# The last 256 columns of an output projection made one tile of 128 at a time, and the results written in smaller pieces from three engines

## The chip, the cores and the metric

The kernel runs on one core of a Trainium2 chip. The metric is the device time of one execution in microseconds (us), as the median of several runs. TensorE (PE in the profile) multiplies, VectorE (DVE), ScalarE (ACT) and GpSimd (POOL) work elementwise, SyncE (SP) starts transfers; ACT can start transfers too, and all transfers share 16 DMA engines.

## The reference, cut to what matters

One layer of a streaming encoder serves 256 prompt rows and 32 sample rows with the same weights (D = 2048). The change concerns its last two lines alone:

```
out = merged @ w_out                      # 288 rows x 2048 @ 2048 x 2048, float32
x   = x + gate * rms_norm(out, g_post)    # mean of squares over the 2048 columns, then 1/sqrt
```

## The kernel before, in words

All 288 rows (`T`) stand side by side as the moving operand, transposed, and weights are the stationary operand, so that a product comes out as tiles of 128 output columns by 288 rows. Each float32 factor is split into a high part and a rest, which gives three products: `hi` by `xh` (L161), `hi` by `xl` (L162) and `lo` by `xh` (L164). `weights` (L137) loads 8 x 128 rows by 256 columns (1 MB, tile `raw`) from SP's queue; `split_weights` (L144) cuts it into two pieces of four 128-row blocks each, `whi` with a copy on ACT (L126) and `wlo` with a subtraction on DVE (L127). `product` (L176) makes 256 columns (`WC`), which are two output tiles, f = 0 and f = 1, in two PSUM tiles `acc`: over four pieces it runs the 12 matmuls of f = 0 and then the 12 of f = 1 for each piece, so both tiles are complete only with the last piece.

The output projection is the loop at L793 over q = 0 to 7, 256 columns each. After the product, each tile is copied to SBUF (`of`, L800, ACT), transposed by PE into the PSUM tiles `aux` (L804 for the two groups of 128 prompt rows, L806 for the samples), squared and summed along its columns by ACT (L810, the sum goes to `so`), and multiplied by the gate `gbc` on DVE (L822) into the result buffers: `t` for the prompts, the second half of `xt` for the samples. At q = 6 DVE sums the seven finished parts of the squares (`sm`, L814 and L815); at q = 7 it adds the last (L817), and GpSimd raises `sm` to the power of -0.5 (`rr`, L819). Then DVE makes `x + t * rr` in one instruction for each half of each prompt group (four of 128x1024) and one for the samples (32x2048, `xt`), all at L828; each result is stored by a transfer that ACT starts (L830: `p % 2` is 0 for all five).

The order on the engines at this point is set by a scheduler from the program's order and its dependences, not by hand. There are four `acc` and four `aux` tiles in PSUM, and four buffers each of `whi` and `wlo`.

Of the kernel before, what the change touches and what calls it, by code (L numbers as in the profile page):

```python
# [10 lines left out]
F32 = mybir.dt.float32  # L11
F32R = mybir.dt.float32r
AF = mybir.ActivationFunctionType
ALU = mybir.AluOpType
PSUM = bass.MemoryType.PSUM

P = 128
# [89 lines left out]
def hybrid_step(ctx: ExitStack, tc, x_prompt, x_sample, c_prompt, c_sample, state_conv, state_ret,  # L107
# [13 lines left out]
    def acc_tile():  # L121
        return acc.tile([P, 512], F32, name="acc", tag="acc")
# [21 lines left out]
    def split_weights(raw):  # L144

        n, width = raw.shape[1:]
        m = min(n, PIECE // width)
        for k in range(0, n, m):
            m = min(m, n - k)
            hi = buffer("whi", PIECE, F32R, PARTS, MORE_PARTS)  # L150
            lo = buffer("wlo", PIECE, F32R, PARTS, MORE_PARTS)
            hi, lo = (t[:, :m * width].rearrange("p (k c) -> p k c", k=m) for t in (hi, lo))
            split(raw[:, k:k + m], hi, lo)
            yield k, hi, lo
# [21 lines left out]
    def product(w, col, xh, xl):  # L176

        out = [acc_tile(), acc_tile()]
        for half in range(2):
            for k, hi, lo in split_weights(weights(w, half * KH, KH, col, WC)):  # L180
                kt = half * KH + k
                for f in range(2):
                    accumulate(out[f][:, :T], hi, lo, f, kt, xh, xl, kt == 0, kt + hi.shape[1] == NK)
                    step()
                    if between and kt == KH and f == 0:
                        between.pop(0)()
            turn[0] += 1
            if turn[0] % 2 == 0:
                next(later, None)
        return [o[:, :T] for o in out]  # L190

    ident = const.tile([P, P], F32, name="ident")
    make_identity(nc, ident)
# [589 lines left out]
    with tc.tile_pool(name="fin", bufs=2, reuse_waits="tile") as fp:  # L783
        so = fp.tile([P, 3, NQ], F32, name="so", bufs=1)
        V.memset(so, 1.0)
        x01 = ybig.tile([P, 2, D], F32, name="x01", tag="yh")
        t01 = pbig.tile([P, 2, D], F32, name="t01", tag="part")
        xt2 = ybig.tile([P, 2, D], F32, name="xt2", tag="yl")
        xs = (x01[:, 0, :], x01[:, 1, :], xt2[:, 0, :])
        ts = (t01[:, 0, :], t01[:, 1, :], xt2[:, 1, :])  # L790
        A.dma_start(out=x01, in_=x_prompt[0].rearrange("(g p) d -> p g d", p=P))
        A.dma_start(out=xs[2][:TS], in_=x_sample[0])
        for q in range(NQ):  # L793
            cols = slice(q * WC, (q + 1) * WC)
            pm = product(w_out[0], q * WC, mh, ml)
            pa, pb = aux_tile(), aux_tile()
            os = []
            for f in range(2):
                o = fp.tile([P, T], F32, name="of")
                A.copy(out=o, in_=pm[f][:, :T])  # L800
                os.append(o)
            for f, o in enumerate(os):
                for g in range(2):
                    nc.tensor.transpose(out=pa[:, g * WC + f * P:g * WC + (f + 1) * P], in_=o[:, g * P:(g + 1) * P], identity=ident)  # L804
            for f, o in enumerate(os):
                nc.tensor.transpose(out=pb[:TS, f * P:(f + 1) * P], in_=o[:, TP:T], identity=ident)  # L806
            src = (pa[:, 0:WC], pa[:, WC:2 * WC], pb[:TS, 0:WC])
            for g in range(3):
                n = rows_of[g]
                A.activation(ts[g][:n, cols], src[g], AF.Square, accum_out=so[:n, g, q:q + 1])  # L810
            if q == NQ - 2:

                sm = fp.tile([P, 3], F32, name="sm", bufs=1)
                V.tensor_reduce(out=sm, in_=so[:, :, :NQ - 1], axis=mybir.AxisListType.X, op=ALU.add)  # L814
                V.tensor_scalar(out=sm, in0=sm, scalar1=1.0 / D, scalar2=EPS, op0=ALU.mult, op1=ALU.add)  # L815
            if q == NQ - 1:
                V.scalar_tensor_tensor(out=sm, in0=so[:, :, q], scalar=1.0 / D, in1=sm, op0=ALU.mult, op1=ALU.add)  # L817
                rr = fp.tile([P, 3], F32, name="rr", bufs=1)
                G.tensor_tensor(out=rr, in0=sm, in1=neghalf, op=ALU.pow)  # L819
            for g in range(3):  # L820
                n = rows_of[g]
                V.tensor_tensor(out=ts[g][:n, cols], in0=src[g], in1=gbc[:n, 0 if g < 2 else 1, cols], op=ALU.mult)  # L822
        outs = (y_prompt[0, 0:P], y_prompt[0, P:TP], y_sample[0])
        W = D // 4
        for g, p, w in ((0, 0, 2), (0, 2, 2), (1, 0, 2), (1, 2, 2), (2, 0, 4)):
            n = rows_of[g]
            c = slice(p * W, (p + w) * W)
            V.scalar_tensor_tensor(out=xs[g][:n, c], in0=ts[g][:n, c], scalar=rr[:n, g:g + 1], in1=xs[g][:n, c],  # L828
                                   op0=ALU.mult, op1=ALU.add)
            (nc.sync if p % 2 else A).dma_start(out=outs[g][:, c], in_=xs[g][:n, c])  # L830


_INS = ["x_prompt", "x_sample", "c_prompt", "c_sample", "state_conv", "state_ret", "ada_w", "ada_b", "norm_pre",
# [28 lines left out]
```

## Time and profile before

| what | value |
|---|---|
| time, median of 3 runs | 1353.85 us (1353.58 to 1354.37) |
| the profiled execution's own time | 1354.2 us |
| its span, first to last instruction | 1352.4 us |
| PE busy | 1324.2 us, 98% of the span |
| DVE, ACT, POOL busy | 834.1, 547.5, 10.0 us |
| moved by DMA | 267.80 MB, mean 198 GB/s |

The span is what the profile's rows cover; 1.8 us of the profiled execution lie outside of it. Rows are given in us from the span's start. A duration of a pipelined instruction runs from its start to its end, so that two neighbours overlap; where a sequence is added up, the distance of starts counts.

### The profile page before, as it was taken

To read this page: it belongs to the slowest core of one execution; us is meant where nothing else is said; L and a number is where in the kernel's file an instruction comes from. 1 tells how busy PE (TensorE), PEld (TensorE's weight loads), DVE (VectorE), ACT (ScalarE), POOL (GpSimd) and SP (SyncE) were. 2 spreads that over 40 slices of the span, in tenths; PEclk is the share of its full clock that TensorE was granted. 3 is DMA by queue.
4 is the path that set the end of the run, shared out by engine and by line. 5 is a ranking of instruction groups with operands and counts; after the bars stand their busy time and mean duration, and the time that the engine had idled before them with its cause. 6 is when DMAs were issued, how large, how long until landed. Compare 5 with 4: busy or idle time off the path is not lost.

```text
span 1352.4 us, 24163 instructions
## 1 busy us (share of the span) xinstructions
PE 1324.2 (98%) x10266; PEld 1302.0 (96%) x10266; DVE 834.1 (62%) x1380; ACT 547.5 (40%) x812; POOL 10.0 (1%) x18
## 2 busy tenths in 40 slices
PE   6999999999999999999999999999999999999996
PEld 5899899999999999999999999999999999999995
DVE  4667679865557766756877875555555544655443
ACT  4443346654444333333333333333333334334441
POOL 0000000000000000000000000000000000000000
PEclk8999999999999999999999999999999999999998
DMA  9988765455455675675666665544546355557431
GB/s 381 376 320 332 298 226 163 129 164 166 144 172 172 211 249 187 200 236 188 199 208 217 203 207 183 180 163 157 183 160 188 126 173 170 157 169 244 156 94 70
DMA packets 209116, 267.80 MB, mean 198 GB/s; under 512 B 5072, under 2 KB 199936, under 8 KB 201872
## 3 DMA queue, kind: packets, MB, share of 16 engines
q1 hardware_dynamic: 202784, 256.13, 55.9%
q10 hardware_dynamic: 6224, 10.13, 2.5%
q8 instruction: 80, 1.31, 0.4%
q14 instruction: 28, 0.23, 0.1%
HBM read 261.75 MB, written 4.49 MB: 197 GB/s over the span
## 4 chain that ended last, share of the span: by engine, by line
PE 96%; DVE 2%; ACT 1%; DMA 1%; issue 0%; DVEq 0%; POOL 0%; POOLq 0%; ACTq 0%
PE acc L162 26%; PE acc L161 26%; PE acc L164 26%; PE pair L374 4%; PE pair L378 4%; PE pair L375 4%; PE small L306 2%; PE aux L665 1%; PE aux L508 0%; PE aux L509 0%; PE aux L510 0%; DVE wlo L289 0%; PE pair L422 0%; PE aux L610 0%; DMA state<-in_state_ret_dram 0%; PE aux L804 0%
## 5 line engine op out<-in xcount | busy, mean ns | idle before, releaser
L127 DVE TENSOR_TENSOR wlo<-raw,whi 128x1024 fp32r<-128x1024 f32 x336 | 410.4, 1222 | 364.6 <-ACT whi L126 364.3
L126 ACT CAST whi<-raw 128x1024 fp32r<-128x1024 f32 x336 | 352.6, 1050 | 518.6 <-PE acc L162 471.3
L161 PE MATMUL acc<-hh,whi 128*128 128x288 f32 x1920 | 524.4, 296 | 0.9 <-DVE firsts L383 0.9
L162 PE MATMUL acc<-hl,whi 128*128 128x288 f32 x1920 | 525.0, 295 | 0.0
L161 PEld LDWEIGHTS acc<-hh,whi 128*128 128x128 f32 x1920 | 360.8, 188 | 1.4 <-ACT whi L126 1.1
L162 PEld LDWEIGHTS acc<-hl,whi 128*128 128x128 f32 x1920 | 361.1, 188 | 0.1
L164 PE MATMUL acc<-hh,wlo 128*128 128x288 f32 x1920 | 329.4, 293 | 0.0
L164 PEld LDWEIGHTS acc<-hh,wlo 128*128 128x128 f32 x1920 | 281.1, 188 | 0.0
L374 PE MATMUL pair<-hh,whi 128*128 128x288 f32 x384 | 110.3, 302 | 2.3 <-ACT hh L346 1.7
L375 PE MATMUL pair<-hl,whi 128*128 128x288 f32 x384 | 109.1, 299 | 0.1
L649 DVE SCALAR_TENSOR_TENSOR gbc<-raw,sc,gbc 128x256 f32<-128x256 f32 x240 | 100.5, 476 | 4.0 <-DMA raw<-in_ada_w_dram 3.9
L383 DVE TENSOR_TENSOR firsts<-pair,firsts 128x576 f32<-128x576 f32 x84 | 62.3, 753 | 39.4 <-PE pair L378 39.3
L378 PE MATMUL pair<-hh,wlo 128*128 128x288 f32 x384 | 84.1, 299 | 1.9 <-DVE wlo L289 1.8
L374 PEld LDWEIGHTS pair<-hh,whi 128*128 128x128 f32 x384 | 73.3, 191 | 5.8 <-issue 2.9
L375 PEld LDWEIGHTS pair<-hl,whi 128*128 128x128 f32 x384 | 73.4, 191 | 0.3 <-DVE hl L352 0.3
L162 PE MATMUL acc<-ml,whi 128*128 128x288 f32 x256 | 70.6, 297 | 0.0
L161 PE MATMUL acc<-mh,whi 128*128 128x288 f32 x256 | 70.1, 296 | 0.0
L161 PE MATMUL acc<-ch,whi 128*128 128x288 f32 x256 | 70.0, 296 | 0.0
L162 PE MATMUL acc<-yl,whi 128*128 128x288 f32 x256 | 70.0, 295 | 0.0
L161 PE MATMUL acc<-yh,whi 128*128 128x288 f32 x256 | 69.9, 296 | 0.0
L162 PE MATMUL acc<-cl,whi 128*128 128x288 f32 x256 | 69.5, 294 | 0.0
L378 PEld LDWEIGHTS pair<-hh,wlo 128*128 128x128 f32 x384 | 63.0, 191 | 3.1 <-DVE wlo L289 3.1
(182 smaller groups left out, 1316.3 us busy)
## 6 DMA issues: line engine op xcount, KB each, us to landing
raw<-in_w_in_dram SPq DMA_DIRECT2D x120, 1024.0 KB
raw<-in_w_branch_dram SPq DMA_DIRECT2D x32, 1024.0 KB
raw<-in_ada_first_dram SPq DMA_DIRECT2D x28, 1024.0 KB
raw<-in_w_first_dram SPq DMA_DIRECT2D x23, 1024.0 KB
raw<-in_ada_w_dram SPq DMA_DIRECT2D x16, 1024.0 KB
raw<-in_w_out_dram SPq DMA_DIRECT2D x16, 1024.0 KB
raw<-in_ada_first_dram SPq DMA_DIRECT2D x8, 512.0 KB
raw<-in_x_prompt_dram SPq DMA_DIRECT2D x2, 1024.0 KB
```

Source lines behind the costliest of these rows:

```text
L126: A.copy(out=hi, in_=src)
L127: V.tensor_tensor(out=lo, in0=src, in1=hi.bitcast(F32), op=ALU.subtract)
L161: nc.tensor.matmul(ps, hi[:, k, fs], xh[:, k0 + k, :], start=first and k == 0, stop=False)
L162: nc.tensor.matmul(ps, hi[:, k, fs], xl[:, k0 + k, :], start=False, stop=False)
L164: nc.tensor.matmul(ps, lo[:, k, fs], xh[:, k0 + k, :], start=False, stop=last and k == n - 1)
L306: nc.tensor.matmul(pm[at:at + 32, :GS * P], cs[:, kt, :], v[:, k, s, :], start=kt < 2, stop=kt >= NK - 2, tile_position=(0, at))
L374: nc.tensor.matmul(ps, hi[:, fs], hh[:, kt, :], start=k == 0, stop=False)
L375: nc.tensor.matmul(ps, hi[:, fs], hl[:, kt, :], start=False, stop=False)
L378: nc.tensor.matmul(ps, lo[:, fs], hh[:, kt, :], start=False, stop=k == GS - 1)
L383: V.tensor_tensor(out=sums, in0=pp[:, :, :T], in1=sums, op=ALU.add)
L649: V.scalar_tensor_tensor(out=ga[:, b], in0=raw[:, k], scalar=sc[:, kt, b:b + 1], in1=ga[:, b], op0=ALU.mult, op1=ALU.add)
L665: nc.tensor.matmul(pg[:, b, :], ones32, ga[:, b, :], start=True, stop=True)
```

## The change

The loop now stops after q = 6. The last 256 columns go through `product_by_tile`: it loads and splits the same four pieces, then runs all 48 matmuls of f = 0, hands that tile out, and runs the 48 of f = 1. Copy, transposes, squares and gate are made for each tile apart, 128 columns wide. At the end the prompts' result is made on DVE in pieces of 512, 768, 768, 1024 and 1024 columns and stored from SP's queue; the samples' result is made in two halves of 1024 columns, the product with `rr` on ACT (Identity with a scale) and the sum with `x` on GpSimd, and stored from ACT's queue.

```diff
+    def product_by_tile(w, col, xh, xl):
+
+        out = [acc_tile(), acc_tile()]
+        pieces = [(half * KH + k, hi, lo) for half in range(2) for k, hi, lo in split_weights(weights(w, half * KH, KH, col, WC))]
+        for f in range(2):
+            for kt, hi, lo in pieces:
+                accumulate(out[f][:, :T], hi, lo, f, kt, xh, xl, kt == 0, kt + hi.shape[1] == NK)
+            yield out[f][:, :T]
...
-        for q in range(NQ):
+        def turned(f, ps, pa, pb):
+
+            o = fp.tile([P, T], F32, name="of")
+            A.copy(out=o, in_=ps)
+            for g in range(2):
+                nc.tensor.transpose(out=pa[:, g * WC + f * P:g * WC + (f + 1) * P], in_=o[:, g * P:(g + 1) * P], identity=ident)
+            nc.tensor.transpose(out=pb[:TS, f * P:(f + 1) * P], in_=o[:, TP:T], identity=ident)
+
+
+        sl = fp.tile([P, 3, 2], F32, name="sl", bufs=1)
+        V.memset(sl, 0.0)
+        for q in range(NQ - 1):
...
+        q = NQ - 1
+        for f, ps in enumerate(product_by_tile(w_out[0], q * WC, mh, ml)):
+            pa, pb = aux_tile(), aux_tile()
+            turned(0, ps, pa, pb)
+            cols = slice(q * WC + f * P, q * WC + (f + 1) * P)
+            src = (pa[:, 0:P], pa[:, WC:WC + P], pb[:TS, 0:P])
+            for g in range(3):
+                n = rows_of[g]
+                A.activation(ts[g][:n, cols], src[g], AF.Square, accum_out=sl[:n, g, f:f + 1])
+            V.scalar_tensor_tensor(out=sm, in0=sl[:, :, f], scalar=1.0 / D, in1=sm, op0=ALU.mult, op1=ALU.add)
+            if f == 1:
                 rr = fp.tile([P, 3], F32, name="rr", bufs=1)
                 G.tensor_tensor(out=rr, in0=sm, in1=neghalf, op=ALU.pow)
             for g in range(3):
                 n = rows_of[g]
                 V.tensor_tensor(out=ts[g][:n, cols], in0=src[g], in1=gbc[:n, 0 if g < 2 else 1, cols], op=ALU.mult)
         outs = (y_prompt[0, 0:P], y_prompt[0, P:TP], y_sample[0])
-        W = D // 4
-        for g, p, w in ((0, 0, 2), (0, 2, 2), (1, 0, 2), (1, 2, 2), (2, 0, 4)):
+        W = D // 8
+
+        def result(g, p, w):
             n = rows_of[g]
             c = slice(p * W, (p + w) * W)
-            V.scalar_tensor_tensor(out=xs[g][:n, c], in0=ts[g][:n, c], scalar=rr[:n, g:g + 1], in1=xs[g][:n, c],
-                                   op0=ALU.mult, op1=ALU.add)
-            (nc.sync if p % 2 else A).dma_start(out=outs[g][:, c], in_=xs[g][:n, c])
+            if g < 2:
+                V.scalar_tensor_tensor(out=xs[g][:n, c], in0=ts[g][:n, c], scalar=rr[:n, g:g + 1], in1=xs[g][:n, c],
+                                       op0=ALU.mult, op1=ALU.add)
+            else:
+                A.activation(ts[g][:n, c], ts[g][:n, c], AF.Identity, scale=rr[:n, g:g + 1])
+                G.tensor_tensor(out=xs[g][:n, c], in0=ts[g][:n, c], in1=xs[g][:n, c], op=ALU.add)
+            (nc.sync if g < 2 else A).dma_start(out=outs[g][:, c], in_=xs[g][:n, c])
+
+        for g, p, w in ((0, 0, 2), (2, 0, 4), (2, 4, 4), (0, 2, 3), (0, 5, 3), (1, 0, 4), (1, 4, 4)):
+            result(g, p, w)
```

The order of the instructions differs from before in the tail alone. On PE, the kernel before ends as follows; acc_14133 is the tile of f = 1 at q = 7, of_14252 and of_14254 are the copies of f = 0 and f = 1.

```order
L161 MATMUL acc_14133<-mh_12156,whi_14222 128x288
L162 MATMUL acc_14133<-ml_12157,whi_14222 128x288
L164 MATMUL acc_14133<-mh_12156,wlo_14223 128x288 x4
L804 MATMUL aux_14250<-ident_67,of_14252 128x128 x2
L806 MATMUL aux_14251<-ident_67,of_14252 32x128
L804 MATMUL aux_14250<-ident_67,of_14254 128x128 x2
L806 MATMUL aux_14251<-ident_67,of_14254 32x128
```

In the changed kernel the place that differs on PE is where f = 0 (acc_14134) ends and f = 1 (acc_14135) begins; of_14206 is the copy of f = 0.

```order
L162 MATMUL acc_14134<-ml_12157,whi_14152 128x288
L164 MATMUL acc_14134<-mh_12156,wlo_14153 128x288 x4
L161 MATMUL acc_14135<-mh_12156,whi_14138 128x288
L162 MATMUL acc_14135<-ml_12157,whi_14138 128x288
L161 MATMUL acc_14135<-mh_12156,whi_14138 128x288
L162 MATMUL acc_14135<-ml_12157,whi_14138 128x288
L807 MATMUL aux_14204<-ident_67,of_14206 128x128 x2
L808 MATMUL aux_14205<-ident_67,of_14206 32x128
L161 MATMUL acc_14135<-mh_12156,whi_14138 128x288
```

The three transposes of f = 0 have moved from the tail to the fifth place of f = 1's accumulation; the tail keeps those of f = 1.

On DVE, the kernel before ends with one gate product for each group, the sum of squares, and the five results.

```order
L822 TENSOR_TENSOR t_13173<-aux,gbc 128x256
L817 SCALAR_TENSOR_TENSOR sm<-so,sm 128x3
L822 TENSOR_TENSOR t_13173<-aux,gbc 128x256
L822 TENSOR_TENSOR xt_13174<-aux,gbc 32x256
L828 SCALAR_TENSOR_TENSOR x_13172<-t_13173,rr,x_13172 128x1024 x4
L828 SCALAR_TENSOR_TENSOR xt_13174<-xt_13174,rr 32x2048
```

In the changed kernel DVE's end from the last column tile on reads:

```order
L847 TENSOR_TENSOR t_13173<-aux,gbc 128x128
L841 SCALAR_TENSOR_TENSOR sm<-sl,sm 128x3
L847 TENSOR_TENSOR t_13173<-aux,gbc 128x128
L847 TENSOR_TENSOR xt_13174<-aux,gbc 32x128
L855 SCALAR_TENSOR_TENSOR x_13172<-t_13173,rr,x_13172 128x512
L855 SCALAR_TENSOR_TENSOR x_13172<-t_13173,rr,x_13172 128x768 x2
L855 SCALAR_TENSOR_TENSOR x_13172<-t_13173,rr,x_13172 128x1024 x2
```

The samples' instruction has left DVE, and the prompts' first piece has half its former columns. On ACT, the changed kernel ends as follows (before, ACT ended with the three squares of 256 columns and five DMA issues).

```order
L805 COPY of<-acc 128x288
L840 ACTIVATE t_13173,sl<-aux 128x128 x2
L840 ACTIVATE xt_13174,sl<-aux 32x128
L858 ACTIVATE xt_13174<-xt_13174,rr 32x1024 x2
L860 DMA out_dram<-xt_13174 32x1024 x2
```

The samples' two products with `rr` have come onto ACT, with their two stores behind them; GpSimd has two sums `xt<-xt` of 32x1024 (L859) behind `rr`, and SP the five prompt stores behind its last weight load.

## Rows read from the trace of the kernel before

**Rows 1.** The page's first part: busy time, share of the span and instructions of each engine.

```profile
PE 1324.2 (98%) x10266; PEld 1302.0 (96%) x10266; DVE 834.1 (62%) x1380; ACT 547.5 (40%) x812; POOL 10.0 (1%) x18
```

**Rows 2.** The chain of waits that ended last, in order of time, over the last 15 us: start, duration, engine and what it worked on.

```profile
1337.63 0.53 PE acc L164 x4
...
1338.24 0.41 ACT of L800
...
1338.69 0.45 PE aux L804 x2
...
1339.16 0.84 ACT t L810 x4
1340.01 0.35 ACT xt L810 x2
...
1340.38 0.17 DVE sm L817
...
1340.66 0.89 POOLq L858
...
1341.57 1.28 DVE x L828
```

**Rows 3.** The timeline of the same stretch: start, duration, engine, line, operation, out<-in, sizes; in brackets the idle time before and who ended it.

```profile
1336.67 0.40 ACT L800 COPY of<-acc 128x288 f32<-128x288 f32 x1 [9.38 <-PE acc L164]
...
1337.98 0.38 PE L804 MATMUL aux<-ident,of 128*128 128x128 f32 x2
...
1340.04 0.42 DVE L822 TENSOR_TENSOR t<-aux,gbc 128x256 f32<-128x256 f32 x1 [11.82 <-ACT t L810]
```

**Rows 4.** The timeline of PE (PEld is its weight load) where the transposes of q = 6 stand between matmuls of q = 7.

```profile
1324.04 0.68 PE L164 MATMUL acc<-mh,wlo 128*128 128x288 f32 x4
...
1324.55 0.38 PE L804 MATMUL aux<-ident,of 128*128 128x128 f32 x2
...
1324.80 0.38 PE L161 MATMUL acc<-mh,whi 128*128 128x288 f32 x1
...
1325.41 0.29 PE L161 MATMUL acc<-mh,whi 128*128 128x288 f32 x1
1325.63 0.20 PEld L804 LDWEIGHTS aux<-ident,of 128*128 128x128 f32 x2 [0.17 <-ACT of L800]
...
1325.94 0.38 PE L162 MATMUL acc<-ml,whi 128*128 128x288 f32 x1
```

**Rows 5.** The timeline of ACT and DVE where the last of the four weight pieces of q = 7 is split.

```profile
1324.23 1.05 ACT L126 CAST whi<-raw 128x1024 fp32r<-128x1024 f32 x1 [0.59 <-PE acc L162]
...
1325.31 1.22 DVE L127 TENSOR_TENSOR wlo<-raw,whi 128x1024 fp32r<-128x1024 f32 x1 [1.94 <-ACT whi L126]
```

**Rows 6.** The instructions of L828 (duration in ns, least, median and most; first and last start), and the four of the prompts in the timeline.

```profile
L828 DVE SCALAR_TENSOR_TENSOR x<-t,rr,x x4: 1276/1277/1283, 1341.6 to 1345.2; 128x1024 f32<-128x1024 f32 x4
L828 DVE SCALAR_TENSOR_TENSOR xt<-xt,rr x1: 2333/2333/2333, 1346.4 to 1346.4; 32x2048 f32<-32x2048 f32 x1
...
1341.57 4.87 DVE L828 SCALAR_TENSOR_TENSOR x<-t,rr,x 128x1024 f32<-128x1024 f32 x4 [0.38 <-POOL rr L819]
```

**Rows 7.** The stores: their issues on ACT's queue in the timeline; then stretches of the span with, behind each, its length, the busy time of PE, PEld, DVE, ACT and POOL, the granted clock of PE, the busy share of the DMA engines and GB/s.

```profile
1342.88 3.92 ACTq L830 DMA_DIRECT2D out_dram<-x  x4
1348.72 0.34 ACTq L830 DMA_DIRECT2D out_dram<-xt  x1
...
1342.88:1343.76 0.88, 0.00 (x0) 0.00 (x0) 0.88 (x1) 0.00 (x0) 0.00 (x0) 0.65 0.00 0
1343.76:1349.10 5.34, 0.00 (x0) 0.00 (x0) 4.93 (x4) 0.00 (x0) 0.00 (x0) 0.50 0.99 393
1349.56:1350.96 1.40, 0.00 (x0) 0.00 (x0) 0.00 (x0) 0.00 (x0) 0.00 (x0) 0.50 0.88 187
1350.96:1352.40 1.44, 0.00 (x0) 0.00 (x0) 0.00 (x0) 0.00 (x0) 0.00 (x0) 0.50 0.00 0
```

**Rows 8.** SP's last weight load: its issue in the timeline, and the stretch of 1 us behind it (columns as in rows 7).

```profile
1299.70 0.37 SPq L141 DMA_DIRECT2D raw<-in_w_out_dram  x1
...
1299.70:1300.70 1.00, 1.00 (x10) 1.00 (x9) 0.58 (x2) 0.72 (x5) 0.00 (x0) 1.00 0.00 0
```

**Rows 9.** Groups of instructions on ACT by line and shape: count, busy us, mean ns of one, idle before.

```profile
L345 ACT ACTIVATE h<-xT,add,mul 128x256 f32<-128x256 f32 x15 | 9.0, 600 | 9.6 <-DVE add L330 9.6
L810 ACT ACTIVATE t<-aux 128x256 f32<-128x256 f32 x16 | 6.0, 381 | 4.4 <-PE aux L804 4.4
L345 ACT ACTIVATE h<-xT,add,mul 128x32 f32<-128x32 f32 x14 | 5.6, 399 | 0.0
L126 ACT CAST vh<-aux 128x512 fp32r<-128x512 f32 x8 | 4.7, 586 | 1.1 <-PE aux L554 1.1
```

**Rows 10.** The same for POOL; these are nearly all that it does.

```profile
L204 POOL TENSOR_TENSOR rstd<-ms,neghalf 128x3 f32<-128x3 f32 x8 | 6.8, 851 | 401.0 <-DVE so L596 341.0 <-DVE ms L202 60.0
L204 POOL TENSOR_TENSOR rstd<-ms,neghalf 128x1 f32<-128x1 f32 x3 | 1.7, 559 | 9.5 <-DVE pick L214 5.3 <-DVE ms L202 4.2
...
masks.py:199 POOL TENSOR_SCALAR_AFFINE_SELECT ident<-ident 128x128 f32<-128x128 f32 x1 | 0.3, 293 | 0.1
masks.py:197 POOL MEMSET ident<- 128x128 f32 x1 | 0.2, 204 | 0.3 <-POOLq L843 0.3
...
L843 POOL MEMSET const-float32-1.0<- 128x1 f32 x1 | 0.1, 99 | 0.0
```

More of the change, by code (lines that the diff above doesn't have):

```diff
@@ L796, in hybrid_step @@
             pa, pb = aux_tile(), aux_tile()
-            os = []
             for f in range(2):
[L799 to L806, printed above, removed]
+                turned(f, pm[f], pa, pb)
             src = (pa[:, 0:WC], pa[:, WC:2 * WC], pb[:TS, 0:WC])
@@ L815, in hybrid_step @@
                 V.tensor_scalar(out=sm, in0=sm, scalar1=1.0 / D, scalar2=EPS, op0=ALU.mult, op1=ALU.add)
-            if q == NQ - 1:
-                V.scalar_tensor_tensor(out=sm, in0=so[:, :, q], scalar=1.0 / D, in1=sm, op0=ALU.mult, op1=ALU.add)
+            for g in range(3):
+                n = rows_of[g]
+                V.tensor_tensor(out=ts[g][:n, cols], in0=src[g], in1=gbc[:n, 0 if g < 2 else 1, cols], op=ALU.mult)
+        q = NQ - 1
[4 more added lines that the diff above has]
+            src = (pa[:, 0:P], pa[:, WC:WC + P], pb[:TS, 0:P])
+            for g in range(3):
+                n = rows_of[g]
+                A.activation(ts[g][:n, cols], src[g], AF.Square, accum_out=sl[:n, g, f:f + 1])
+            V.scalar_tensor_tensor(out=sm, in0=sl[:, :, f], scalar=1.0 / D, in1=sm, op0=ALU.mult, op1=ALU.add)
+            if f == 1:
                 rr = fp.tile([P, 3], F32, name="rr", bufs=1)
```

## The prediction

> **What bounds the kernel now.** I read the busy times first: PE works for 98% of the span [rows 1], so an edit can only count where PE waits, or has finished. The change touches the last 15 us. The chain of waits there shows the second place: PE's last accumulation ends at 1338.16, and from then on one engine works at a time [rows 2]: ACT copies (to 1338.65), PE transposes (to 1339.14), ACT squares (to 1340.36), DVE and POOL make `rr` (to 1341.55), and from 1341.57 DVE makes the results. I call this start S. S lies 3.41 us behind PE's last accumulation. Then the stores: the first is issued when DVE's first piece is done, its data moves from 1343.76, and the 16 DMA engines are 99% busy at 393 GB/s until 1349.10 [rows 7]. DVE makes a prompt piece of 512 KB in 1.20 us from start to start ((1345.2-1341.6)/3, [rows 6]), 437 GB/s, a little faster than the stores drain. The samples' 256 KB come last: DVE needs 2.33 us for them [rows 6], so the DMA engines stand idle for 0.46 us, and then move them at 187 GB/s in 1.40 us. From there to the span's end it is 1.44 us [rows 7]. So the tail has three sections: PE's end to S (bound by a chain), S to the first data (one DVE piece and one issue), first to last data (7.20 us; bound by DMA, and at its end by DVE).
>
> **The change part by part.**
>
> *PE, f = 0's transposes.* Before, they lie under the copy of f = 1: from 1337.98, done long before that copy lets the next ones start [rows 3, 2]; they cost nothing. Now they stand in the midst of f = 1's matmuls, with the whole of PE's stream behind them. Matmuls start every 0.13 us (0.53 for four, rows 2). At q = 6 three transposes lengthen the distance of two matmuls to 0.37 (1324.80 less 1324.43, the fourth start of that L164 group), 0.24 more, where their copy was ready, and to 0.53, 0.40 more, where PE waited 0.17 for it [rows 4]. The new ones stand four matmuls, 0.52 us, behind f = 0's last; its copy is ready 0.53 us (1338.69 less 1338.16) behind that matmul's end, which lies 0.16 behind the start of the next. So there is a wait of about 0.17 again. I take **+0.40**; ends +0.24 and +0.55.
>
> *The order of matmuls.* f = 0 now takes a weight piece every 1.58 us instead of every 3.16, so the last piece is needed three pieces behind the start of q = 7 at 1324.80, at about 1329.9. It is split by 1326.53 (1325.31 plus 1.22, [rows 5]): 3.4 us of cover, and no cost. Without that cover PE would wait for the difference. Copy, squares and gate of f = 0 lie under f = 1's 6.3 us on engines that had idled 9.4 and 11.8 us there [rows 3].
>
> *PE's end to S.* The three squares have 128 columns less each. ACT from PSUM takes 381 ns for 256 columns and 586 for 512, 0.80 ns a column [rows 9], so 0.10 each: **-0.31**; ends -0.20 (part of it fixed) and -0.35. The first gate product on DVE stands ahead of the sum; it shrinks as well (from 0.42, rows 3) and stays beside the third square. S becomes 1341.57+0.40-0.31 = 1341.66.
>
> *First store.* DVE takes 1277 ns for 1024 columns and 2333 for 2048, 1.03 ns a column, so 749 for 512: **-0.53**. The store moves to SP's queue, which has nothing else left. SP's last load shows no byte for 1.00 us behind its issue [rows 8], ACT's first store 0.88 [rows 7]: **+0.16** with the 1.04 I take; ends 0 and 0.2. First data at S+1.82 (0.75 and 0.03 to the issue).
>
> *DVE.* Starts follow each other 0.08 closer than the durations; pieces of 512, 768, 768, 1024, 1024 start at S, 0.67, 1.60, 2.53 and 3.73, and the last ends at **S+5.01**. Before it was 1348.69, S+7.12: the samples' 2.33 have left it. The last store's data can move from S+6.08.
>
> *Samples.* ACT's product of 1024 columns with a scale: L345 gives 0.90 ns a column and 370 fixed, 1.29 us; a plain copy 1.05 [rows 5, 9]; I take 1.25. GpSimd's sum of 1024 columns has no row. Its fill of 128 columns takes 204 ns against 99 for one, 0.82 ns a column, which would be 0.94 us for the sum; its select, one read and one write, 293 ns, 1.5 a column, 1.6 us; with two reads twice that, 3.2 us [rows 10]. Two columns more of the power cost 292 ns, 146 each, which would be 150 us; that is a function's price and not a sum's, and I leave it out. I take 2.3, between select and twice select. Then the halves are ready at S+3.6 and S+5.9, and the second one's data can move at S+6.8, while the last prompt store moves. This path sets nothing as long as its last data moves by S+7.4. The Trainium skill (GPSIMD Engine Reference, section "3.1 Elementwise — side-by-side cycle accounting") gives 4497 ns for a sum of 2048 float32 columns; halved, an estimate of 2.25 us, by which the sum would not change. No row here shows it.
>
> *First to last data.* The bytes are the same 2.36 MB; at 393 GB/s they need 6.0 us. The second store comes 0.26 late (its piece ends at S+1.68, data at S+2.75, the first is moved by S+2.49); after that data always waits. So 6.3 us where it was 7.20: **-0.90**; ends -1.2 (no gap) and -0.5 (the samples' last half on its own at 187 GB/s, 0.70 us). The drain is now the bound, and DVE's last piece, done 2 us before its last byte, is not.
>
> *Sum.* +0.40-0.31-0.53+0.16-0.90 = **-1.18 us**; with all the ends taken together -1.8 to -0.3. The profiled execution has a span of 1352.4 and 1354.2 of its own time, so 1351.2 and 1353.0; that execution lies 0.35 over the median, so for the median 1353.85-1.18 = **1352.65**, own range 1352.1 to 1353.5.
>
> **The rivals.**
>
> *DVE and GpSimd keep each other from SBUF.* Both read two operands from SBUF at that moment, L855 its `t` and `x`, L859 its product and `x`. No row of before has the two engines so at once: GpSimd's powers run while DVE waits for them, and the last one beside products that read one operand from PSUM. If only one of them can read at a time, DVE's 5.0 us and GpSimd's 4.6 stand in line. With the sums in between: the first asks at S+1.3, runs from the end of DVE's second piece at 1.68 to 3.98, the third piece to 4.99, the second sum to 7.29, the last pieces to S+9.77; then 1.07 to data, 1.33 for 512 KB, 1.44 to the end: S+13.6 = 1355.3, **+2.9**, 1356.7. With both sums behind DVE: S+9.6, 0.91 to data, 0.70, 1.44: S+12.65 = 1354.3, **+1.9**, 1355.75. With a sum of 1.6 us it would be 1.4 less. It decides from the point at which DVE's last piece is 0.7 us late (data over by S+8.1), and the gain is gone at 1.9 us. For it: the operands; against it: nothing but that no row shows it. This is the case on the other side: 34%, 1355.4 to 1356.8, likeliest 1356.3. The Trainium skill (SBUF — State Buffer, section "Who interferes with whom") speaks for it: a DVE instruction with two SBUF inputs contends with a GpSimd instruction that reads SBUF, and the one that issues first holds the shared ports for its whole length. By that rule the first time of this paragraph would come out; the trace cannot agree or disagree.
>
> *They only slow each other*, each by a part: between both cases, about +0.7, 1354.5: 12%.
>
> *GpSimd's sum is slow.* At 3.2 us, without any quarrel, the halves end at S+4.5 and S+7.7, the last data moves from S+8.6 for 0.7: S+10.75, 1352.4, no change, 1353.85: 10%. That is the edit that takes work off DVE and puts as much on a slower path.
>
> *The change does less than it says*: the scheduler could have left f = 0's transposes at the end; its order shows that it did not. They could gain nothing where the copy is late: if ACT were busy, PE would wait there longer, up to 0.5 more; ACT has no piece left to split then [rows 5], so I give it no chance of its own.
>
> **How the numbers follow.** The forecast has 44%, the rivals 34, 12 and 10. A change of 0.2%, 2.7 us, is about what a measurement of this kernel can tell from none. Faster than 1351.1 would need more than all ends on the good side: 3%. Slower than 1356.55 holds about a third of the first rival and a little for what I have not thought of: 14%. The rest, 83%, is within. The range reaches from the forecast's low side, 1351.9, to the first rival's high side, 1356.8; no more than 1 in 10 is outside.
>
> **What the profile of the changed kernel would show.** PE's last accumulation about 0.4 later than 1338.16; S 3.1 behind it; the first prompt piece 0.75 us long, five pieces without idle time between, the last done 5.0 us behind S; sums of GpSimd near 2.3 us each beside them; the DMA engines busy from S+1.8 to S+8.1 with one short gap. If a prompt piece of DVE starts late or lasts 2 us and more, or a sum of GpSimd lasts far over 2.3 while DVE works, the first rival has it. If the sums last over 3 us and DVE is undisturbed, it is the slow sum. A last weight piece that PE waits for, or a first store that takes much over 1 us to its data, would make the sum wrong at a place where I see no reason for it.

## The result and the profile after

The changed kernel takes 1357.04 us (median of 17 runs, 1356.28 to 1358.07) and the kernel before 1354.34 on the same chip (17 runs, 1353.44 to 1355.62): ratio 1.0021, interval 1.0015 to 1.0028. It is slower by 2.7 us. The forecast was 1352.65; the time lies just above the range, and what came is the first rival. The profiled execution has a span of 1354.49 where before's has 1352.41.

The busy times, with [rows 1] beside them, show it in one place only: PE, DVE and ACT differ by 3 us or less, and POOL has gained 5.7 us with two instructions more.

```profile
PE 1324.2 (98%) x10266; PEld 1301.6 (96%) x10266; DVE 837.1 (62%) x1385; ACT 550.0 (41%) x820; POOL 15.7 (1%) x20
```

The chain of waits of the last 15 us (start, duration, engine and what it worked on), to be read with [rows 2]:

```profile
1337.98 0.54 PE acc L164 x4
...
1338.60 0.41 ACT of L805
...
1339.05 0.45 PE aux L807 x2
...
1339.53 0.63 ACT t L840 x4
1340.15 0.24 ACT xt L840 x2
...
1340.73 0.85 POOL rr L844
...
1341.61 0.75 DVE x L855
1342.36 0.93 DVEq L891
1343.29 7.49 DVE x L855 x3
```

Up to the start of the results, S, the links are those of before. PE ends at 1338.51 (1337.98 plus 0.54, less 0.01 of rounding) and S is 1341.61, so it is 3.10 us long and was 3.42. The two squares of the prompts and that of the samples take 0.63 and 0.24 where they took 0.84 and 0.35. The new thing is the last line: three pieces of DVE last 7.49 us.

DVE's pieces one by one in the timeline (start, duration, line, out<-in, sizes; in brackets the idle time before):

```profile
1341.61 0.75 DVE L855 SCALAR_TENSOR_TENSOR x<-t,rr,x 128x512 f32<-128x512 f32 x1 [0.65 <-POOL rr L844]
1342.28 1.01 DVE L855 SCALAR_TENSOR_TENSOR x<-t,rr,x 128x768 f32<-128x768 f32 x1
1343.21 3.10 DVE L855 SCALAR_TENSOR_TENSOR x<-t,rr,x 128x768 f32<-128x768 f32 x1
1346.23 3.35 DVE L855 SCALAR_TENSOR_TENSOR x<-t,rr,x 128x1024 f32<-128x1024 f32 x1
1349.51 1.27 DVE L855 SCALAR_TENSOR_TENSOR x<-t,rr,x 128x1024 f32<-128x1024 f32 x1
```

and GpSimd's two sums in the same stretch:

```profile
1342.83 2.66 POOL L859 TENSOR_TENSOR xt<-xt 32x1024 f32<-32x1024 f32 x1 [1.26 <-ACT xt L858]
1345.46 3.04 POOL L859 TENSOR_TENSOR xt<-xt 32x1024 f32<-32x1024 f32 x1
```

Lay the ends side by side. DVE's second piece ends at 1343.29; the first sum, which was there since 1342.83, ends 2.20 later, at 1345.49. DVE's third piece, there since 1343.21, ends 0.82 after that, at 1346.31. The second sum ends 2.19 after that (1348.50), the fourth piece 1.08 after that (1349.58). Each engine finishes one instruction while the other stands: they take turns, by whole instructions. Two pieces of the same shape differ by a factor of about three (768 columns: 1.01 and 3.10; 1024 columns: 1.27 and 3.35), so it is not the pieces' own work.

The stores follow. In stretches of the span (behind each its length, the busy time of PE, PEld, DVE, ACT and POOL, PE's clock, the busy share of the DMA engines and GB/s):

```profile
1343.24:1345.00 1.76, 0.00 (x0) 0.00 (x0) 1.76 (x2) 0.55 (x1) 1.76 (x1) 0.70 0.88 339
1345.00:1347.20 2.20, 0.00 (x0) 0.00 (x0) 2.20 (x2) 0.00 (x0) 2.20 (x2) 0.50 0.37 96
1347.20:1350.40 3.20, 0.00 (x0) 0.00 (x0) 3.20 (x2) 0.00 (x0) 1.30 (x1) 0.50 0.48 157
1350.40:1353.18 2.78, 0.00 (x0) 0.00 (x0) 0.38 (x1) 0.00 (x0) 0.00 (x0) 0.50 0.94 377
1353.18:1354.49 1.31, 0.00 (x0) 0.00 (x0) 0.00 (x0) 0.00 (x0) 0.00 (x0) 0.50 0.00 0
```

In [rows 7] the DMA engines had 5.34 us without a gap at 393 GB/s; now they wait for data in the middle, at 96 and 157 GB/s. The last data moves at 1353.18, 11.57 us behind S (9.40 before). So the 2.07 us of the two spans are: S later by 0.04 (PE's end +0.36, the way from there to S -0.32), S to last data +2.17, last data to end -0.13.

### The profile page after: what moved, and what is told of

It is laid out like the page before. It is cut to its first block, busy times and chain, and to the rows that moved or that the text cites. A ratio compares the mean times of both kernels' runs of the same rounds, so it can differ in the third digit from the quotient of the medians.

```text
span 1354.5 us, 24188 instructions
## 1 busy us (share of the span) xinstructions
PE 1324.2 (98%) x10266; PEld 1301.6 (96%) x10266; DVE 837.1 (62%) x1385; ACT 550.0 (41%) x820; POOL 15.7 (1%) x20
## 4 chain that ended last, share of the span: by engine, by line
PE 96%; DVE 2%; ACT 1%; DMA 1%; issue 0%; POOL 0%; DVEq 0%; POOLq 0%; ACTq 0%
PE acc L161 26%; PE acc L162 26%; PE acc L164 26%; PE pair L383 4%; PE pair L387 4%; PE pair L384 4%; PE small L315 2%; DVE x L855 1%; PE aux L674 1%; PE aux L517 0%; PE aux L518 0%; PE aux L519 0%; DVE wlo L298 0%; PE pair L431 0%; PE aux L807 0%; PE aux L619 0%
```

## The experiments

In the expectations, theory A is that VectorE's and GpSimd's instructions with operands in SBUF exclude each other for their whole length; theory B is that the stores or ScalarE's product hold VectorE up. Where an excerpt of a diff leaves lines out, `...` stands for them.

**Both kernels a second time.**

> The kernel before, unchanged, for a second profile. In the profiles so far a group of 12 matmuls of the output projection takes 1568 and 1591 ns in turn in the kernel before, and 1600 in the changed one in the loops that the change left alone; over five loops that is 0.78 us. If that belongs to the run and not to the program, this profile shows loops between 13.42 and 13.60 us in another mixture; if it belongs to the program, 13.43 us again.

> The changed kernel, unchanged, for a second profile beside that of the kernel before on the same chip. Theory A: the same lengths to 0.05 us: pieces of 0.75, 1.01, 3.1, 3.4 and 1.27 us, sums of 2.66 and 3.04; last store's data over 11.5 us behind the first piece's start. The loops of the output projection: 13.59 us each if the slower groups of 12 matmuls belong to the program, a mixture of 13.42 to 13.60 if to the run.

The kernel before: span 1352.5, last data 9.40 us behind S. The changed one: 1354.6, the two long pieces 3.10 and 3.36, last data 11.56 behind S. The collision repeats to 10 ns. The loops that these two expectations ask about are told below, under TensorE's pace.

**The samples' sum back on VectorE.**

```
-                G.tensor_tensor(out=xs[g][:n, c], in0=ts[g][:n, c], in1=xs[g][:n, c], op=ALU.add)
+                V.tensor_tensor(out=xs[g][:n, c], in0=ts[g][:n, c], in1=xs[g][:n, c], op=ALU.add)
...
-        for g, p, w in ((0, 0, 2), (2, 0, 4), (2, 4, 4), (0, 2, 3), (0, 5, 3), (1, 0, 4), (1, 4, 4)):
+        for g, p, w in ((0, 0, 2), (0, 2, 3), (2, 0, 4), (0, 5, 3), (2, 4, 4), (1, 0, 4), (1, 4, 4)):
```

> One edit to the changed kernel: the samples' sum goes from GpSimd to VectorE (two of 32x1024, placed behind the second and the third prompt piece); everything else stays, the product on ScalarE, the pieces, SyncE's queue, the tile-by-tile projection. Theory A (VectorE's and GpSimd's instructions that both read two operands from SBUF exclude each other for their whole length): the prompt pieces last 0.75, 1.01, 1.01, 1.28, 1.28 us again, the sums 1.22 each as VectorE's 128x1024 subtraction does; VectorE ends 7.3 us behind its first piece, the span 11.1 behind it, 1.7 us less than with GpSimd and 0.3 to 0.5 over the kernel before: ratio to before 1.0003. Theory B (the stores from two queues in smaller pieces, or ScalarE's product, are what holds VectorE up): pieces of 3 us remain, ratio 1.0015 and more.

Measured 1355.31, ratio to before 1.0009 (1.0000 to 1.0018); the changed kernel's is 1.0021. The sums cost VectorE 1.20 us each, the prompts' pieces are 0.75, 1.01, 1.00 and 1.27 again, and the last data moves 9.65 us behind S. When GpSimd has no sums to make, 1.92 of the 2.17 us that the changed kernel loses between S and the last data are gone, though VectorE has more to do. The product on ScalarE and the seven stores are the same, two of them in another place, and the long pieces of theory B do not come. In time 1.3 of the 2.7 us are left, with an interval that reaches down to nothing. There is no gain: the stores need 8.01 us from first to last data. VectorE's pieces, then the whole drain:

```profile
L855 DVE SCALAR_TENSOR_TENSOR x<-t,rr,x x5: 752/1010/1267, 1342.2 to 1348.2; 128x768 f32<-128x768 f32 x2, 128x1024 f32<-128x1024 f32 x2, 128x512 f32<-128x512 f32 x1
...
1343.82:1351.83 8.01, 0.00 (x0) 0.00 (x0) 5.62 (x6) 0.55 (x1) 0.00 (x0) 0.50 0.82 294
```

**What of GpSimd's instruction keeps VectorE waiting?** Three kernels, one run each. In the first GpSimd only writes (fills over the product, which is stored; the samples' result is left out):

```
-                G.tensor_tensor(out=xs[g][:n, c], in0=ts[g][:n, c], in1=xs[g][:n, c], op=ALU.add)
-            (nc.sync if g < 2 else A).dma_start(out=outs[g][:, c], in_=xs[g][:n, c])
+                for _ in range(2):
+                    G.memset(ts[g][:n, c], 0.0)
+            (nc.sync if g < 2 else A).dma_start(out=outs[g][:, c], in_=(xs if g < 2 else ts)[g][:n, c])
```

> The changed kernel with GpSimd's two sums replaced by four fills with zero of 32x1024 at the same place behind ScalarE's product (so the samples' result is left out): GpSimd writes SBUF, but reads nothing. Theory A in its narrow form (what they share is reading): fills of 0.9 to 1.0 us each, VectorE's pieces undisturbed, last piece done 5.0 us behind the first one's start, span about 9.5 us behind that start. A wider form (any GpSimd instruction on SBUF excludes VectorE's): a piece or two of VectorE's lasts 1 to 2 us longer, last piece done 8 to 9 us behind the start. Theory B (stores): 9.2 us as in the changed kernel.

In the second it copies, with one operand (the samples' result leaves out `x`):

```
-                G.tensor_tensor(out=xs[g][:n, c], in0=ts[g][:n, c], in1=xs[g][:n, c], op=ALU.add)
+                G.tensor_copy(out=xs[g][:n, c], in_=ts[g][:n, c])
```

> The changed kernel with GpSimd's two sums replaced by copies of 32x1024 (one operand read from SBUF; the samples' result leaves out x). Theory A: a GpSimd instruction that reads one operand excludes VectorE's two-operand pieces just as well, for its own length, which I estimate at 1.0 to 1.6 us from the select of 128 columns; VectorE's last piece is done 5.0 us plus both copies behind the first start, 7 to 8 us, and one or two pieces last as much longer as a copy lasts. If two operands on both sides are needed: pieces undisturbed, done at 5.0.

In the third GpSimd has its sums, and VectorE takes one operand from SBUF only: its second is a zeroed PSUM bank `zt`, so the prompts' results leave out `x`; eight pieces of 512 columns.

```
+        zt = acc_tile()
+        V.memset(zt, 0.0)
...
-                V.scalar_tensor_tensor(out=xs[g][:n, c], in0=ts[g][:n, c], scalar=rr[:n, g:g + 1], in1=xs[g][:n, c],
+                V.scalar_tensor_tensor(out=xs[g][:n, c], in0=ts[g][:n, c], scalar=rr[:n, g:g + 1], in1=zt[:n, :512],
...
```

> The changed kernel with VectorE's second operand taken from PSUM (a bank filled with zero beforehand) instead of x in SBUF, so the prompts' result leaves out x; since a bank holds 512 columns there are eight pieces of 128x512. GpSimd's two sums stay as they are. Theory A: VectorE reads one operand from SBUF, GpSimd's sums run beside it at their own pace, 2.2 us each, from 1.25 to 5.7 us behind the start; VectorE's pieces last 0.75 to 0.85 us each and are done 5.5 us behind the start; span 9.5 to 9.8 us behind it. Theory B, or a wider exclusion: pieces that last 2 us and more beside the sums, VectorE done at 9 to 10 us.

The times were 1354.68, 1354.54 and 1354.58, single runs. The evidence is in the durations (ns: least, median, most). GpSimd only writes:

```profile
L855 DVE SCALAR_TENSOR_TENSOR x<-t,rr,x x5: 752/1011/1278, 1342.1 to 1345.9; 128x768 f32<-128x768 f32 x2, 128x1024 f32<-128x1024 f32 x2, 128x512 f32<-128x512 f32 x1
...
L860 POOL MEMSET xt<- x4: 941/941/941, 1343.3 to 1346.2; 32x1024 f32 x4
```

GpSimd copies:

```profile
L855 DVE SCALAR_TENSOR_TENSOR x<-t,rr,x x5: 751/1272/2050, 1342.5 to 1347.8; 128x768 f32<-128x768 f32 x2, 128x1024 f32<-128x1024 f32 x2, 128x512 f32<-128x512 f32 x1
...
L859 POOL COPY xt<-xt x2: 1362/1560/1759, 1343.7 to 1345.0; 32x1024 f32<-32x1024 f32 x2
```

VectorE reads one operand from SBUF:

```profile
L857 DVE SCALAR_TENSOR_TENSOR x<-t,rr,acc x8: 741/741/748, 1342.2 to 1346.8; 128x512 f32<-128x512 f32 x8
...
L861 POOL TENSOR_TENSOR xt<-xt x2: 2336/2342/2349, 1343.5 to 1345.8; 32x1024 f32<-32x1024 f32 x2
```

Beside writes, VectorE's longest piece is 1278 ns, its own length. Beside a copy it is 2050, with 0.77 us of waiting. Beside a sum, but with one operand from PSUM, all eight pieces are alike and GpSimd's sums alike at 2.34 us. So in these runs it takes two things at once: a VectorE instruction with two operands in SBUF, and a GpSimd instruction that reads SBUF, be it one operand or two. The sums' own time, 2.34, is what the prediction took (2.3), so the rival of the slow sum is out.

These kernels also show what the change would have been worth without the collision. VectorE is done 5.00 us behind S in the first, as forecast, but the last data moves 9.43 behind S (first) and 9.22 (third), not the 8.1 of the sum.

**The parts apart.** The last column tile by output tile, with the results as before:

> The first part of the change alone: the last 256 columns tile by tile, the results as in the kernel before (four prompt pieces and the samples on VectorE, all stores from ScalarE). My sum gives +0.40 us for the moved transposes and -0.31 for the narrower squares: VectorE's first piece 0.0 to 0.1 us later against the kernel before, the tail behind it as before; span 1352.5, ratio 1.0000. If the moved transposes or the other order of the matmuls cost more than I saw, 1.0005 and more, and it shows between TensorE's last accumulation of the sixth 256 columns and its last of all.

1354.9, ratio 1.0005 (0.9996 to 1.0014); S is 3.10 behind PE's end, last data 9.39 behind S. And the changed results alone, with the last column tile as before:

> The kernel before with the changed results alone: seven pieces in the changed order, the samples' product on ScalarE and sum on GpSimd, the prompts' stores on SP, and the last column tile as before (two output tiles at once). If the loss lies in the results: two VectorE pieces of 3.1 and 3.4 us, last data at 11.6 us behind the start of the results (before 9.40), start of the results 3.42 us behind TensorE's last accumulation as before, so 2.2 us over the kernel before, ratio 1.0016. If the new order of the last column tile is needed for the collision (its half-width last products leave VectorE at another moment), the pieces stay at 1.01 and 1.28 us and the ratio is 1.000. TensorE's loops 2 to 6 tell whether their 13.59 us (before 13.45) comes with the code of the last column tile (then 13.45 here) or with any other change of the program (then 13.59).

1356.30 against 1354.05, ratio 1.0014 (1.0005 to 1.0024), so 2.2 us over. The two engines' instructions read as in the changed kernel:

```profile
L830 DVE SCALAR_TENSOR_TENSOR x<-t,rr,x x5: 752/1274/3355, 1341.9 to 1349.8; 128x768 f32<-128x768 f32 x2, 128x1024 f32<-128x1024 f32 x2, 128x512 f32<-128x512 f32 x1
...
L834 POOL TENSOR_TENSOR xt<-xt x2: 2653/2848/3042, 1343.2 to 1345.8; 32x1024 f32<-32x1024 f32 x2
```

Last data is 11.57 behind S, and S 3.42 behind PE's end. So the collision and 2.2 of the 2.7 us come with the results alone. The new order of the last column tile is 0.9 us over before, with an interval from -0.5 to +1.9: these runs can't tell it from nothing. In its profile the way from PE's end to the last data is 0.33 shorter; the moved transposes and slower loops, told below, stand against that.

**A version without the second engine.** A cheaper way to take the samples' 2.33 us from VectorE: an instruction's price goes by columns, so four blocks of 512 columns side by side on 128 partitions cost one piece of 512. The samples' columns of each output tile are kept in `sf`, four tiles are transposed at once (in q = 6 and 7), and a small matmul with `mf` adds the four blocks' sums of squares:

```
-            for f, o in enumerate(os):
-                nc.tensor.transpose(out=pb[:TS, f * P:(f + 1) * P], in_=o[:, TP:T], identity=ident)
+                V.tensor_copy(sf[:, kt % 4, kt // 4, :], pm[f][:, TP:T])
...
+                    nc.tensor.transpose(out=pb[:, f * P:(f + 1) * P], in_=sf[:, 2 * h + f].rearrange("p j r -> p (j r)"), identity=ident)
...
+        for g, p, w in ((0, 0, 2), (2, 0, 0), (0, 2, 3), (0, 5, 3), (1, 0, 4), (1, 4, 4)):
...
+                V.scalar_tensor_tensor(out=xs2, in0=ts2, scalar=rr[:, 2:3], in1=xs2, op0=ALU.mult, op1=ALU.add)
+                for ps, cs_ in fold:
+                    A.dma_start(out=y_sample[0][:, cs_], in_=xs2[ps])
```

> The projection as before the change (two tiles of 128 columns at a time), prompts' results and stores as in the changed kernel, and the samples neither on GpSimd nor as 32 rows of 2048: VectorE gathers each tile's 32 sample columns, four 128x128 transposes (two at the sixth, two at the last 256 columns) replace sixteen of 128x32, so that the samples lie as 128 partitions x 512 (four groups of 32 rows); a 128x128 matrix of ones and zeros sums the squares over the four groups; the result is one VectorE instruction of 128x512 and four stores of 32x512 from ScalarE. Theory A with the second point (samples' stores of 32 partitions move at half the rate): prompt pieces 0.75, 1.01, 1.01, 1.28, 1.28 us, the samples' 0.75; VectorE ends 5.7 us behind its first start, the stores drain near 390 GB/s and are over 8.0 to 8.3 us behind it instead of 9.4; TensorE saves about 0.2 us in each of six loops; 2 to 3 us under the kernel before, ratio 0.998. If only GpSimd mattered and the drain does not depend on the samples' shape: the stores end at 9.0 to 9.4 and it is 1 to 1.5 us under, ratio 0.999. If the gathering costs more than the transposes give: 1.000 and more.

1353.48 against 1353.79, ratio 0.9998 (0.9989 to 1.0007): no difference. VectorE's pieces were short and undisturbed (5.67 us in all), and the last data moved 9.14 behind S. The samples' four stores stood in the second place, and behind them the DMA engines had too little to do for a while:

```profile
1343.50:1344.00 0.50, 0.00 (x0) 0.00 (x0) 0.50 (x1) 0.00 (x0) 0.00 (x0) 0.50 0.60 139
```

So two things were changed at once: the samples' piece went behind the prompts' third, and VectorE takes the samples' columns from ScalarE's copy (except at q = 7), where in folded that copy had waited for VectorE:

```
-                V.tensor_copy(sf[:, kt % 4, kt // 4, :], pm[f][:, TP:T])
-                A.copy(out=o, in_=pm[f][:, :TP])
+                    A.copy(out=o, in_=pm[f][:, :T])
+                    V.tensor_copy(sf[:, kt % 4, kt // 4, :], o[:, TP:T])
...
-        for g, p, w in ((0, 0, 2), (2, 0, 0), (0, 2, 3), (0, 5, 3), (1, 0, 4), (1, 4, 4)):
+        for g, p, w in ((0, 0, 2), (0, 2, 3), (0, 5, 3), (2, 0, 0), (1, 0, 4), (1, 4, 4)):
```

> The folded kernel with its two faults mended: the samples' piece on VectorE (four blocks of 512 columns side by side on 128 partitions, as in folded) stands behind the prompts' third piece instead of behind the first, and in column tiles 0 to 6 VectorE takes the samples' columns from ScalarE's copy in SBUF instead of from the PSUM tile that ScalarE copies. If the stores starved in folded because the samples' four small stores stood in the second place, the drain has no gap now: start of the results 3.3 us behind TensorE's last accumulation, first data at +1.6, then 6.0 us for the bytes at 393 GB/s and 0.7 more because the samples' bytes, from 32 partitions at a time, move at half rate: last data at +8.3 (folded +9.14, before +9.40), so 1 us under the kernel before, ratio 0.9992, if TensorE's loops stay at 13.45 us; up to 0.8 us less of a gain if they take 13.59. If the drain is bound by something else that all these kernels share, last data stays at +9.1 to +9.4 and the ratio at 0.9998 or over.

1352.52 against 1354.05, ratio 0.9989 (0.9980 to 0.9998): 1.5 us faster than before, with an interval of 0.3 to 2.7; set beside the 2.7 us that the change costs, it is about 4 us faster than the change, which was not run beside it. It is the only version that beats both. In the timeline VectorE has nothing between the pieces but work:

```profile
1340.10 2.61 DVE L857 SCALAR_TENSOR_TENSOR x<-t,rr,x 128x512 f32<-128x512 f32 x3 [0.36 <-POOL rr L847]
1342.63 0.75 DVE L861 SCALAR_TENSOR_TENSOR xt<-xt,rr 128x512 f32<-128x512 f32 x1
1343.29 2.48 DVE L857 SCALAR_TENSOR_TENSOR x<-t,rr,x 128x1024 f32<-128x1024 f32 x2
```

S to last data is 8.83 (1340.10 to 1348.93), 0.57 under before, where 8.3 was expected. From PE's end to S it is 3.27, 0.15 less than before. PE ends at 1336.83, 1.3 us earlier than before's 1338.15, but its projection began 0.54 earlier, which is the scatter told below. From there to PE's end it is 106.1 us, before 106.9. Fewer transposes do not explain these 0.8: folded has as few and needs 107.1. In the profiles PE's weight loads wait for ScalarE's copies for 1.0 us in all before, 1.6 in folded and 0.3 here, and folded has the slower loops that are told below; what is worth how much was not told apart. In stretches, two half microseconds and the whole drain:

```profile
1343.00:1343.50 0.50, 0.00 (x0) 0.00 (x0) 0.50 (x2) 0.00 (x0) 0.00 (x0) 0.50 1.00 387
...
1345.00:1345.50 0.50, 0.00 (x0) 0.00 (x0) 0.50 (x1) 0.00 (x0) 0.00 (x0) 0.50 0.95 205
...
1341.74:1348.93 7.19, 0.00 (x0) 0.00 (x0) 4.03 (x5) 0.00 (x0) 0.00 (x0) 0.57 0.91 328
```

The DMA engines are as busy at 1345.0, where the samples' stores move, as at 1343.0 with prompts, but carry half: 205 and 387 GB/s. That is the same half rate that [rows 7] show for the samples' store of before, 187. So a store from 32 partitions at a time paid it in both places, at the end and among others. The Trainium skill (SBUF — State Buffer, section "Door 1: The DMA port swizzle") says that a range of 32 partitions reaches 8 of the 16 ports, and gives 189 GB/s for it, measured with transfers of 1 MiB; the trace agrees with 187 for 256 KB.

**TensorE's pace.** Loops of column tiles 2 to 6 are longer in the profile of the changed kernel, though neither the order of any engine's instructions nor what they wait for differs there, and PE's granted clock is 1.00 in both. The starts of one transpose in two consecutive loops in PE's timeline, before:

```profile
1297.68 0.27 PE L804 MATMUL aux<-ident,of 128*128 128x128 f32 x1
...
1311.12 0.27 PE L804 MATMUL aux<-ident,of 128*128 128x128 f32 x1
```

and after:

```profile
1297.09 0.27 PE L807 MATMUL aux<-ident,of 128*128 128x128 f32 x1
...
1310.68 0.27 PE L807 MATMUL aux<-ident,of 128*128 128x128 f32 x1
```

13.44 and 13.59 us. The distance is 13.47 in results_alone, which keeps the loops of before, and 13.46 to 13.47 in the second profile of the kernel before. But the changed kernel's second profile has both paces in one execution: two of the loops 2 to 6 take 13.43 us and three 13.57 to 13.59, the mixture that its expectation had as the sign that the pace belongs to the run. Two loops in succession there, as stretches with the same instructions on PE, DVE and ACT:

```profile
1270.20:1283.62 13.42, 13.42 (x104) 13.24 (x103) 5.98 (x7) 6.06 (x13) 0.00 (x0) 1.00 0.48 156
1283.62:1297.20 13.58, 13.58 (x104) 13.39 (x103) 5.98 (x7) 6.07 (x13) 0.00 (x0) 1.00 0.51 156
```

What differs ahead of these loops is one small tile more, with a fill by VectorE. So the tile and its fill alone in the kernel before, unused:

```
+        sl = fp.tile([P, 3, 2], F32, name="sl", bufs=1)
+        V.memset(sl, 0.0)
```

> The kernel before with nothing but the changed kernel's new small tile for the last squares (3 by 2 columns) and VectorE's fill of it ahead of the output projection; nothing uses it. In column tiles 1 to 6 the instructions of every engine, their order and their waits are the same in the kernel before and in the changed one; this fill and the shift of the tiles behind it are all that differs ahead of the last column tile. If they set TensorE's pace, loops 2 to 6 take 13.58 to 13.60 us here in most places (before 13.42 to 13.47), and the time is 0.5 to 0.8 us over the kernel before. If the pace comes from the last column tile's code, they take 13.42 to 13.47.

and the changed kernel without them, with a longer `so`:

```
-        so = fp.tile([P, 3, NQ], F32, name="so", bufs=1)
+        so = fp.tile([P, 3, NQ + 1], F32, name="so", bufs=1)
...
-        sl = fp.tile([P, 3, 2], F32, name="sl", bufs=1)
-        V.memset(sl, 0.0)
```

> The changed kernel without that tile and its fill: the last squares' sums go into the tile of the other squares' sums, made one column longer. If the fill and the shift behind it set the pace, loops 2 to 6 take 13.42 to 13.47 us and the time is 0.5 to 0.8 us under the changed kernel; else 13.58 to 13.60. The results' two long VectorE pieces of 3.1 and 3.4 us stay either way.

The tile alone:

```profile
1296.95 0.27 PE L806 MATMUL aux<-ident,of 128*128 128x128 f32 x1
...
1310.54 0.27 PE L806 MATMUL aux<-ident,of 128*128 128x128 f32 x1
```

The change without it:

```profile
1297.65 0.27 PE L807 MATMUL aux<-ident,of 128*128 128x128 f32 x1
...
1311.23 0.27 PE L807 MATMUL aux<-ident,of 128*128 128x128 f32 x1
```

13.59 and 13.58: both have the slower pace, in all five loops. So neither the code of the last column tile nor the fill is needed for it. The expectation of no_fill took the shift to be gone with the tile, but it is not: what both share with the changed kernel is, by the sizes in the code, that the tiles behind `so` lie 24 or 12 bytes per partition further on. Every profile with that shift has three to five slow loops among the five, and the three profiles with the tiles in their old places (before twice, results_alone) have none. That the shift is the cause is not shown: one and the same program runs both paces, fill_alone and no_fill could be slow for different reasons, and nothing here says why matmuls that don't read these tiles should go by it. It is no tax on the total that these runs can prove: the five loops add 0.75 us in the first pair of profiles and 0.3 in the second, single runs gave 1353.91 with the tile and 1354.91 without, and the start of the output projection itself scatters by 1.4 us between profiled executions (1230.1 to 1231.5).

## Why the prediction was wrong, step by step

**S behind PE's end.** Right: -0.31 forecast, -0.32 measured; the whole is 3.10 as stated.

**f = 0's transposes within PE's stream.** Right, a little low: +0.40 forecast. In the timeline, PE and its weight load:

```profile
1331.85 0.29 PE L162 MATMUL acc<-ml,whi 128*128 128x288 f32 x1
1332.16 0.44 PE L807 MATMUL aux<-ident,of 128*128 128x128 f32 x2
...
1332.46 0.38 PE L161 MATMUL acc<-mh,whi 128*128 128x288 f32 x1
```

```profile
1332.16 0.20 PEld L807 LDWEIGHTS aux<-ident,of 128*128 128x128 f32 x2 [0.25 <-ACT of L805]
```

From 1331.85 to 1332.46 it is 0.61, 0.48 more than the usual 0.13, with a wait of 0.25 for the copy where 0.17 was taken. No weight piece was waited for. PE's end moved by +0.36 in the two profiled executions, but that is a sum of the +0.48, the slower pace (about +0.9 over six loops, q = 7's part included) and an output projection that happened to start 1.0 earlier. The prediction had no term for the pace; its cause stays open.

**First store.** Right in sign, a little better: the piece took 0.75, and the first data came at S+1.63, where 1.82 was forecast. SP's queue took 0.85 us from issue to data, where 1.04 was taken.

**DVE undisturbed, S+5.01.** Right as a price and wrong as a forecast. Without GpSimd's reads it is 5.00; with them S+9.17.

**Which case.** This is the step that failed: the forecast let DVE's pieces and GpSimd's sums run side by side without a price, and the runs showed them taking turns, which put DVE's end 4.17 us later (S+9.17 for S+5.00). The forecast got 44% and the exclusion 34%, with the words that nothing spoke against it but that no row showed it. The operands were known, and the rule of the Trainium skill (SBUF — State Buffer, section "Who interferes with whom") described this pair of instructions; the trace now agrees with it, down to whole turns, and with its exception for a GpSimd instruction that only writes. I should have taken the exclusion as the likeliest. Its own working was close: S+9.77 for VectorE's end and S+12.17 for the last data, measured 9.17 and 11.57. It put full durations in line; in the trace each of the four turns is 0.15 to 0.2 shorter than the instruction alone (2.19 for 2.34, 0.82 for 1.01, 1.08 for 1.28), together 0.7 us.

**First to last data, 7.20 to 6.3.** Mis-sized, and hidden behind the collision. gpsimd_writes and one_operand, with VectorE undisturbed, needed 7.80 and 7.59. I took 393 GB/s for all bytes, while [rows 7] show 187 for the samples'. Their 0.26 MB cost 0.7 us more at that rate, before as after: the change only puts them beside prompts, and they take the engines from those. With that and the forecast's gap of 0.26 it would be 6.0+0.7+0.26 = 7.0; the other 0.6 to 0.8 lie in dips of supply and the last small stores, and were not told apart. So this term was -0.90 and should have been about +0.5, mostly paid by the first data, which comes 0.56 earlier behind S than before. Without the collision the change would have been worth about nothing in the tail instead of -1.18, as gpsimd_writes' 9.43 from S to last data (9.40 before) shows. No rival of the prediction had that case for this reason.

**The time.** +2.07 in the spans and +2.7 in the medians, for the +2.9 of the rival. That the totals come so close is in part luck. From S to the span's end the rival had 13.6 us where before has 10.84, 2.8 more; measured is 12.88, 2.04 more. The slower loops, about 0.9 in this profile, about made up for the difference, and no part of the prediction had them. The ends of the forecast's terms add up to -1.8 and -0.5, not to the -0.3 that it gives; nothing hangs on it. The range ended 0.24 us below the result because it was built on the 1353.85 of the runs shown, while the kernel before took 1354.34 beside the changed one: 1353.85+2.7 would have been 1356.55.

## What to carry to other kernels

Before work is moved to GpSimd beside VectorE, look where both take their operands. In these runs a VectorE instruction with two operands in SBUF and a GpSimd instruction that reads SBUF ran in turns, so that VectorE, rid of 2.3 us of work, was done 2.05 us later than before (S+9.17 for S+7.12) and not 2.1 earlier. With one operand from PSUM, or with a GpSimd instruction that only writes, there were no turns. If the work has few partitions, folding it onto all of them can shrink it without a second engine: here the samples' piece went from 2.33 us to 0.75, though of the two folded versions only one came out faster than before. And a drain is to be costed store by store with the rate that the rows show for that shape, not with the rate of the large ones.

## What the runs showed of the hardware that I had not expected

A GpSimd copy with a single operand blocks VectorE as a sum does (pieces of 1.79 and 2.05 us for 1.01 and 1.28), for its own shorter time. The turns are by whole instructions, each 0.15 to 0.2 us shorter than the instruction alone. And loops of the same matmuls in the same order ran at two paces, 13.42 to 13.47 and 13.57 to 13.60 us, at the same granted clock and within one execution; the slower one came in none of the three profiles whose small tiles lie as before's do, and the cause stays open.
